# Halves of TensorE's columns in a recurrence, single weight buffers, and a first chunk in small pieces

## The chip, the core and the metric

The kernel runs on one core of a Trainium2 chip. TensorE (PE in the profile; its weight loads are PEld) multiplies, ScalarE (ACT) and VectorE (DVE) prepare operands and take results out of PSUM, GpSimd (POOL) helps with elementwise work, and SyncE (SP) issues nearly all DMAs. The metric is the device time of one execution in microseconds, as the median of several runs. All weights and inputs lie in HBM, and are float32.

## What is computed

One layer of a hybrid decoder block on 256 tokens of 2048 features. Cut to what matters:

```python
h = rmsnorm(x, norm_mix_g)
u = h @ w_in                                   # 2048 x 12288, ten fields
ya = b_g * causal_dwconv3(c_g * xa) * silu(za) # short convolution branch
o  = hgrn2_chunked(silu(q), kk, iv, log_f)     # gated linear recurrence, 8 heads of 128
yb = rmsnorm_per_head(o) * silu(og)
m  = sigmoid(ga) * (ya @ w_a_out) + sigmoid(gb) * (yb @ w_b_out)
x  = x + m @ w_o
x  = x + sigmoid(rmsnorm(x) @ w_ple_gate) * (p @ w_ple_proj)
return rmsnorm(x, final_norm_g)
```

The product of p, (256 x 256) by (256 x 2048), is the only one that needs no other result, and the kernel begins with it.

## The kernel before, in words

**The stream of weights.** Every weight matrix is cut by the host into groups of 512 output columns, and each group into chunks of 256 rows. A chunk is one *position* of a stream: a tile of 128 partitions by 1024 float32 (512 KB), whose left and right 512 columns belong to two blocks of 128 rows. `steps` (lines 139 to 144) lists the positions in order: four for p's projection (PP 0 to 3, one chunk each), then w_in with w_a and w_b between its last groups, then w_o and w_ple_gate.

**One position.** `load` (line 94) has SP fetch the raw float32 chunk; raw tiles hold two positions (1 MB), and there are three of them. `split` (line 113) makes two operands of a chunk: ScalarE rounds it to `whi` (line 124), VectorE subtracts to get the remainder `wlo` (line 125). The activations are kept as such a pair as well: `put_p` (line 905) makes p's with a cast and a subtraction on VectorE, `put_x` (line 839) x's. `product` (line 952) issues three matmuls per block of 128 rows and half of the tokens: hi by hi, hi by lo, lo by hi (line 957). So a position is twelve matmuls with 512 columns each. Two banks of PSUM hold the two halves of the tokens.

**The order of the work.** The main loop (line 960) walks the positions. At each it splits positions up to three ahead (line 971), issues the twelve matmuls, asks for the weight tiles up to AHEAD = 4 further on (line 1007), and lets each pending epilogue take one step (`advance`). From position 1 to 4 the splits are held behind the eviction of an earlier product (line 970). Epilogues write to DRAM and read back turned (`turned`, lines 233 and 235), also on SP's queue, so these stand in one line with the weight loads.

**The beginning.** SP fetches p whole (line 154, 256 KB), then the right half of position 0 (line 111, 256 KB; its left half goes out on ScalarE's queue), position 1 (512 KB), the parameters `prm` (line 158, 36 KB), and then positions 2 to 5 and the first chunks of x in turn (lines 827 to 829). Meanwhile TensorE runs ten matmuls on zeros (WARM, line 836), which VectorE has just written (line 833). Position 0 is split in two halves of 512 columns (line 973), after its half of p. Its first block issues its matmuls in the order hi by hi, lo of p by hi, hi by lo of the weights (line 1000); all other blocks go through the three kinds for one half of the tokens and then for the other.

**The recurrence.** For each of two groups of four heads (`hgrn`, line 351) small products within blocks of 128 tokens are made by `products` (line 385): at level B, key rows r multiply query columns c. Each product uses a strip of 32 of TensorE's 128 columns (`quarters`, line 378, yields r in strips of 32; `tile_position=(0, r)` places it). At level 128 a strip covers 64 query columns, at all others 32. Line 519 makes the products between the two blocks in the same manner, with 128 query columns for each strip of 32. These operands are plain float32, and each such matmul appears in the profile as two instructions.

Of the kernel before, what the change touches and what calls it, by code (L numbers as in the profile page):

```python
# [15 lines left out]
P = 128  # L16
# [10 lines left out]
WARM = 10  # L27
# [17 lines left out]
def hybrid_kernel(ctx, tc, xT, x, pT, prm, gfin, masks, w_in, w_a, w_b, w_o, w_pg, w_pp, out):  # L45
# [48 lines left out]
    def load(pos):  # L94
        w, g, c = stream[pos]
        if pos // 2 not in loaded:
            raw = wp.tile([P, 2, 2 * CW], F32, tag="raw", bufs=3, name=nm("raw"))
            loaded[pos // 2] = raw
            if FIRST <= pos < FIRST + 4:
                for i in range(2):  # L100
                    nc.sync.dma_start(out=raw[:, i, :], in_=w[g, :, c + i, :])
            elif pos >= FIRST:
                nc.sync.dma_start(out=raw, in_=w[g, :, c : c + 2, :])
        return loaded[pos // 2]

    def load_first(pos, queues):

        w, g, c = stream[pos]
        n = 2 * CW // len(queues)
        for i, eng in enumerate(queues):  # L110
            eng.dma_start(out=load(pos)[:, pos % 2, i * n : (i + 1) * n], in_=w[g, :, c, i * n : (i + 1) * n])

    def split(pos, halves=(0, 1)):
        w, g, c = stream[pos]
        src = load(pos)[:, pos % 2, :]
# [7 lines left out]
        s = slice(halves[0] * CW, (halves[-1] + 1) * CW)  # L123
# [25 lines left out]
    LEAD, AHEAD = 3, 4  # L149
# [4 lines left out]
    nc.sync.dma_start(out=praw.rearrange("p (k t) -> p k t", k=2), in_=pT)  # L154
# [3 lines left out]
    nc.sync.dma_start(out=prm_t, in_=prm)  # L158
# [192 lines left out]
    def hgrn(j):  # L351
# [26 lines left out]
        def quarters(B):  # L378

            for r in range(0, P, 32):  # L380
                c = {128: (r // 64 ^ 1) * 64, 64: r ^ 32}.get(B, r)
                n = max(B // 2, 32)
                yield slice(r, r + 32), slice(c, c + n)

        def products(bk, key, query, B, at=None):

            for h in range(4):
                for r, c in quarters(B):
# [131 lines left out]
        for h in range(4):  # L520
            for r in range(0, P, 32):
                nc.tensor.matmul(  # L522
                    heads(bo)[r : r + 32, h, :], X[:, 0, h, r : r + 32], X[:, 1, h, :], start=True, stop=True,
                    tile_position=(0, r),
                )
# [301 lines left out]
    for c in range(4):  # L827
        load_first(c + 2, (nc.sync,))
# [3 lines left out]
    warm = pools["tmp1"].tile([P, 4, P], F32, tag="both", bufs=1, name="warm")  # L832
    nc.vector.memset(warm[:, :2, :], 0.0)
# [302 lines left out]
```

## Time and profile before

| | |
|---|---|
| time, median of 3 runs | 826.04 us (825.71 to 826.06) |
| the profiled execution, its own time | 826.27 us |
| its span, first to last instruction | 824.5 us |
| mean granted TensorE clock | 0.996 |
| HBM read, written | 172.92 MB, 13.63 MB |

The span is shorter than the execution's own time by 1.8 us, which lie before the first and after the last instruction. An instruction's row in a timeline gives its start in us from the beginning of the span, its length in us, the engine and the line, what it writes and reads, and how many neighbouring instructions of the same kind were merged into the row; in square brackets stands how long the engine had been idle and what released it. SPq and ACTq are the queues on which SP and ACT issue DMAs. Matmul durations overlap: a matmul of 512 columns lasts 0.39 us in its row, while the next one starts some 0.23 us after it.

### The profile page before, as it was taken

How to read it: one execution, taken by the hardware profiler on the slowest of the kernel's cores; microseconds unless marked ns; L12 is line 12 of the kernel's file. 1: busy time of each engine (PE TensorE's matmuls, PEld its weight loads, DVE VectorE, ACT ScalarE, POOL GpSimd, SP SyncE). 2: the span in 40 equal slices, each digit the busy share in tenths (PEclk: the TensorE clock that was granted, in tenths of full speed). 3: DMA queues.
4: the chain of work that ended last, by engine and by line, in shares of the span. 5: the costliest groups of instructions: out<-in, count | busy, mean ns of one | idle time of the engine just before them, and what ended most of it. 6: DMA issues, size and time to landing. Idle time of an engine off the chain costs nothing.

```text
span 824.5 us, 10669 instructions
## 1 busy us (share of the span) xinstructions
PE 814.2 (99%) x4186; PEld 673.6 (82%) x4186; DVE 531.5 (64%) x618; ACT 432.9 (53%) x557; POOL 90.7 (11%) x74
## 2 busy tenths in 40 slices
PE   9999999999999999999999999999999999999995
PEld 6888888888888888888888888888888888888885
DVE  6747698967766588877645546545544656679633
ACT  7667465555564465466443443544444455566522
POOL 1000045300000064200001001000000000001210
PEclk9999999999999999999999999999999999999998
DMA  9969656648776565748656755756755788887702
GB/s 342 378 254 337 221 186 209 217 151 260 256 229 229 200 204 163 246 156 283 207 182 188 262 188 174 254 200 204 246 181 191 249 291 279 302 296 270 295 1 104
DMA packets 40660, 187.27 MB, mean 227 GB/s; under 512 B 4640, under 2 KB 14112, under 8 KB 22432
## 3 DMA queue, kind: packets, MB, share of 16 engines
q1 hardware_dynamic: 40176, 185.52, 65.8%
q10 hardware_dynamic: 432, 1.05, 0.3%
q8 instruction: 33, 0.54, 0.3%
q14 instruction: 19, 0.16, 0.1%
HBM read 172.92 MB, written 13.63 MB: 226 GB/s over the span
## 4 chain that ended last, share of the span: by engine, by line
PE 96%; issue 1%; DMA 1%; DVE 0%; ACT 0%; SPq 0%; POOLq 0%; POOL 0%
PE g L957 94%; PE s L389 1%; PE s L957 1%; DMA raw<-in_w_pp 1%; PE s L522 0%; PE s L546 0%; PE s L545 0%; PE s L544 0%; ACT xs L782 0%; DVE wlo L125 0%; ACT whi L124 0%; DVE t L753 0%; DVE t L757 0%; DVE xs L756 0%; POOLq L1131 0%
## 5 line engine op out<-in xcount | busy, mean ns | idle before, releaser
L125 DVE TENSOR_TENSOR wlo<-raw,whi 128x1024 fp32r<-128x1024 f32 (+1 forms) x293 | 368.0, 1261 | 254.4 <-ACT whi L124 253.8
L124 ACT ACTIVATE whi<-raw 128x1024 fp32r<-128x1024 f32 (+1 forms) x293 | 307.6, 1056 | 334.4 <-PE g L957 294.6
L957 PE MATMUL g<-whi,xl 128*128 128x512 f32 (+1 forms) x912 | 351.4, 385 | 0.0
L957 PE MATMUL g<-wlo,xh 128*128 128x512 f32 (+1 forms) x912 | 351.4, 385 | 0.0
L957 PE MATMUL g<-whi,xh 128*128 128x512 f32 (+1 forms) x912 | 351.3, 386 | 0.0
L957 PEld LDWEIGHTS g<-whi,xh 128*128 128x128 f32 x912 | 171.3, 188 | 34.7 <-issue 0.4
L957 PEld LDWEIGHTS g<-whi,xl 128*128 128x128 f32 x912 | 171.3, 188 | 34.3
L957 PEld LDWEIGHTS g<-wlo,xh 128*128 128x128 f32 x912 | 171.3, 188 | 34.1
L957 PE MATMUL g<-whi,mh 128*128 128x512 f32 x128 | 49.8, 390 | 0.0
L957 PE MATMUL g<-wlo,mh 128*128 128x512 f32 x128 | 49.7, 389 | 0.0
L957 PE MATMUL g<-whi,ml 128*128 128x512 f32 x128 | 49.5, 390 | 0.0
L677 POOL TENSOR_TENSOR t<-ga,gb 128x512 f32<-128x512 f32 x6 | 10.6, 1786 | 198.3 <-DVE gb L672 198.3
L957 PEld LDWEIGHTS g<-whi,mh 128*128 128x128 f32 x128 | 24.0, 188 | 5.3 <-ACT mh L683 0.3
L957 PE MATMUL g<-wlo,yaTh 128*128 128x512 f32 x72 | 28.0, 392 | 0.1
L957 PEld LDWEIGHTS g<-whi,ml 128*128 128x128 f32 x128 | 23.9, 188 | 5.1 <-DVE ml L684 0.2
L957 PEld LDWEIGHTS g<-wlo,mh 128*128 128x128 f32 x128 | 24.0, 188 | 5.0
L957 PE MATMUL g<-whi,yaTl 128*128 128x512 f32 x72 | 27.9, 389 | 0.0
L443 POOL TENSOR_TENSOR t<-b 128x512 f32<-128x512 f32 x10 | 20.4, 2035 | 68.1 <-DMA t<-turn 41.0
L957 PE MATMUL g<-whi,yaTh 128*128 128x512 f32 x72 | 27.8, 391 | 0.0
L957 PE MATMUL g<-whi,ybTh 128*128 128x512 f32 x64 | 24.9, 389 | 0.0
L957 PE MATMUL g<-wlo,ybTh 128*128 128x512 f32 x64 | 24.9, 389 | 0.0
L957 PE MATMUL g<-whi,ybTl 128*128 128x512 f32 x64 | 24.9, 389 | 0.0
(157 smaller groups left out, 516.5 us busy)
## 6 DMA issues: line engine op xcount, KB each, us to landing
raw<-in_w_in SPq DMA_DIRECT2D x93, 1024.0 KB, 5.1
raw<-in_w_o SPq DMA_DIRECT2D x16, 1024.0 KB, 5.9
raw<-in_w_pg SPq DMA_DIRECT2D x16, 1024.0 KB, 5.6
turn<-t SPq DMA_DIRECT2D x72, 128.0 KB, 2.6
t<-turn SPq DMA_DIRECT2D x18, 512.0 KB, 5.2
raw<-in_w_a SPq DMA_DIRECT2D x8, 1024.0 KB, 5.2
raw<-in_w_b SPq DMA_DIRECT2D x8, 1024.0 KB, 5.1
raw<-in_w_in SPq DMA_DIRECT2D x6, 512.0 KB, 7.8
```

Source lines behind the costliest of these rows:

```text
L124: a = nc.scalar.activation(out=hi[:, s], in_=src[:, s], func=AF.Copy)
L125: v = nc.vector.tensor_tensor(out=lo[:, s], in0=src[:, s], in1=hi[:, s].bitcast(F32), op=ALU.subtract)
L389: nc.tensor.matmul(heads(bk)[r, h, c if at is None else slice(at, at + 32)], key(h)[:, r], query(h)[:, c], start=True, stop=True, tile_pos ...
L443: nc.gpsimd.tensor_tensor(out=er, in0=br, in1=ref, op=ALU.subtract)
L677: (nc.vector if j == 3 else nc.gpsimd).tensor_tensor(out=spread(m, t), in0=blocks(ga[:, s]), in1=blocks(gb[:, s]), op=ALU.add)
L957: nc.tensor.matmul(psum, a, b, start=first and n == 0, stop=last and n == 2)
```

## The change

Three edits, with some that follow from them.

- **Recurrence.** `quarters` becomes `places`: at level 128 the strip is 64 of TensorE's columns instead of 32, so there are two products per head instead of four; levels 64 and below keep strips of 32. The products between the two blocks (line 519) use strips of 64 as well.
- **Weight buffers.** Six raw tiles of one position (512 KB) in place of three of two (1 MB), and one DMA per position throughout. The distance AHEAD becomes 5.
- **The beginning.** p is fetched in two halves of 128 KB, position 0 in four pieces of 128 KB, over SP's and ScalarE's queues by turns; position 1 in two pieces of 256 KB on SP's. `prm` goes out after position 2. Position 0 is split in pieces of 256, 256 and 512 columns, position 1 in two of 512. The second half of p is prepared only after the first two pieces are split. The first block of position 0 makes its matmuls for 256 columns at a time (twelve of 256 in place of six of 512). TensorE's warming-up is seven matmuls instead of ten, on a constant of ones that the program holds anyway, and VectorE's memset for it goes.

```diff
-WARM = 10
+WARM = 7
+EARLY = {0: ((0, CW // 2), (CW // 2, CW), (CW, 2 * CW)), 1: ((0, CW), (CW, 2 * CW))}
...
     def load(pos):
         w, g, c = stream[pos]
-        if pos // 2 not in loaded:
-            raw = wp.tile([P, 2, 2 * CW], F32, tag="raw", bufs=3, name=nm("raw"))
...
+        if pos not in loaded:
+            raw = loaded[pos] = wp.tile([P, 2 * CW], F32, tag="raw", bufs=6, name=nm("raw"))
+            if pos >= FIRST:
+                nc.sync.dma_start(out=raw, in_=w[g, :, c, :])
+        return loaded[pos]
...
-    LEAD, AHEAD = 3, 4
+    LEAD, AHEAD = 3, 5
...
-    nc.sync.dma_start(out=praw.rearrange("p (k t) -> p k t", k=2), in_=pT)
-    load_first(0, (nc.scalar, nc.sync))
-    load_first(1, (nc.sync,))
+    load_p(0)
+    n = CW // 2
+    load_columns(0, 0, n, nc.scalar)
+    load_columns(0, n, CW, nc.sync)
+    load_p(1, nc.scalar)
+    load_columns(0, CW, CW + n, nc.sync)
+    load_columns(0, CW + n, 2 * CW, nc.scalar)
+    for n in range(2):
+        load_columns(1, n * CW, (n + 1) * CW, nc.sync)
...
-            for r in range(0, P, 32):
-                c = {128: (r // 64 ^ 1) * 64, 64: r ^ 32}.get(B, r)
-                n = max(B // 2, 32)
-                yield slice(r, r + 32), slice(c, c + n)
+            n = max(B // 2, 32)
+            for r in range(0, P, n):
+                c = r ^ n if B > 32 else r
+                yield slice(r, r + n), slice(c, c + n)
...
-            for r in range(0, P, 32):
+            for r in range(0, P, 64):
                 nc.tensor.matmul(
-                    heads(bo)[r : r + 32, h, :], X[:, 0, h, r : r + 32], X[:, 1, h, :], start=True, stop=True,
+                    heads(bo)[r : r + 64, h, :], X[:, 0, h, r : r + 64], X[:, 1, h, :], start=True, stop=True,
                     tile_position=(0, r),
                 )
...
     for c in range(4):
-        load_first(c + 2, (nc.sync,))
+        load_columns(c + 2, 0, 2 * CW, nc.sync)
+        if c == 0:
+            nc.sync.dma_start(out=prm_t, in_=prm)
         load_x(c)
...
-    nc.vector.memset(warm[:, :2, :], 0.0)
...
+    ones = [nc.const_aps.tensor(1.0, [P, n], mybir.dt.bfloat16) for n in (P, CW)]
...
-            if done == 0:
-                for i in range(2):
-                    put_p(i)
-                    split(done, (i,))
-            else:
+            for c0, c1 in EARLY.get(done, ((0, 2 * CW),)):
+                if done == 0 and c0 % CW == 0:
+                    with ExitStack() as first:
+                        for i in state["splits"] if c0 else ():
+                            first.enter_context(tc.issue_after(i))
+                        put_p(c0 // CW)
                 for k in range(2 * (done - 4), min(2 * (done - 4) + 2, KT)) if done >= 4 else ():
                     put_x(k)
-                split(done)
+                split(done, c0, c1)
...
-            s = slice(i * CW, (i + 1) * CW)
-            for n in ((0,), (2,), (1,)) if pos == 0 and i == 0 else ((0, 1, 2),):
-                for t in range(NT):
-                    product(psum[t], state[opname], k, t, hi[:, s], lo[:, s], k == 0, k == 2 * nch - 1, n)
+            for c0, c1 in EARLY[0][:2] if pos == 0 and i == 0 else ((0, CW),):
+                s = slice(i * CW + c0, i * CW + c1)
+                for n in ((0,), (2,), (1,)) if pos == 0 and i == 0 else ((0, 1, 2),):
+                    for t in range(NT):
+                        product(
+                            psum[t][:, c0:c1], state[opname], k, t, hi[:, s], lo[:, s], k == 0 and c0 == 0, k == 2 * nch - 1, n
+                        )
```

More of the change, by code (lines that the diff above doesn't have):

```diff
@@ L95, in load, with split @@
         w, g, c = stream[pos]
[L96 to L115 removed]
+        if pos not in loaded:
[3 more added lines that the diff above has]
+        return loaded[pos]
+    def split(pos, c0=0, c1=2 * CW):
+        w, g, c = stream[pos]
+        src = load(pos)
         pool, n = (pools["late"], 6) if (pos - state.get("late", len(steps))) % 10 < 6 and "late" in state else (wp, 4)
```

17 lines of the change are left out of this document (9 added, 8 removed).

## The prediction

> **What bounds the kernel now.** I read the page first, for the engine that is full, then the chain of waits in order of time, for the places where that engine is held up, and then the timeline of those places.
>
> ```profile
> span 824.5 us, 10669 instructions
> PE 814.2 (99%) x4186; PEld 673.6 (82%) x4186; DVE 531.5 (64%) x618; ACT 432.9 (53%) x557; POOL 90.7 (11%) x74
> ```
>
> TensorE is busy for 814.2 of 824.5 us. So a change counts only if it lets TensorE start its real products earlier, spares it a stall, or changes the length of what it does. The chain says where these are:
>
> ```profile
> 1.65 5.18 DMA raw<-in_w_pp
> ...
> 6.85 1.07 ACT whi L124
> ...
> 7.94 1.24 DVE wlo L125
> ...
> 9.22 2.57 PE g L957 x10
> 11.79 5.44 PE s L957 x24
> 17.23 119.68 PE g L957 x528
> ...
> 162.92 1.01 PE s L522 x32
> ...
> 176.70 0.22 PE s L544 x2
> ```
>
> Up to 9.22 us the end is set by the landing of position 1 and its two conversions; from there on the chain runs on TensorE until the tail. A product takes 119.68 / 528 = 0.227 us. The change touches two places of this chain: the stretch before 11.63 us, where position 2 begins, and the recurrence's small products.
>
> **The beginning.** The timeline of the first 12 us, weight loads and other queues left out:
>
> ```profile
> 1.19 4.38 PE L837 MATMUL s<-warm 128*128 128x512 bf16 x10 [1.19 <-DVE warm L833]
> ...
> 4.69 0.49 DVE L909 CAST yaTh<-t 128x256 fp32r<-128x256 f32 x2 [3.56 <-DMA t<-in_pT]
> ...
> 4.87 1.29 ACT L124 ACTIVATE whi<-raw 128x512 fp32r<-128x512 f32 x2 [2.19 <-DMA raw<-in_w_pp]
> ...
> 5.54 0.69 DVE L125 TENSOR_TENSOR wlo<-raw,whi 128x512 fp32r<-128x512 f32 x1
> ...
> 5.55 0.73 PE L957 MATMUL g<-whi,yaTh 128*128 128x512 f32 x2
> ...
> 6.48 0.68 DVE L125 TENSOR_TENSOR wlo<-raw,whi 128x512 fp32r<-128x512 f32 x1
> ...
> 7.27 0.44 PE L957 MATMUL g<-wlo,yaTh 128*128 128x512 f32 x1
> ...
> 8.26 1.06 ACT L124 ACTIVATE whi<-raw 128x1024 fp32r<-128x1024 f32 x1 [0.35 <-DMA raw<-in_w_pp]
> ...
> 8.48 0.63 PE L957 MATMUL g<-whi,yaTh 128*128 128x512 f32 x2
> ...
> 9.22 0.50 PE L957 MATMUL g<-wlo,yaTh 128*128 128x512 f32 x1
> ...
> 9.35 1.23 DVE L125 TENSOR_TENSOR wlo<-raw,whi 128x1024 fp32r<-128x1024 f32 x1 [0.18 <-ACT whi L124]
> ...
> 9.56 0.39 PE L957 MATMUL g<-whi,yaTl 128*128 128x512 f32 x1
> ...
> 11.63 0.39 PE L957 MATMUL s<-whi,yaTh 128*128 128x512 f32 x1
> ...
> 11.86 0.39 PE L957 MATMUL s<-wlo,yaTh 128*128 128x512 f32 x1
> ```
>
> VectorE and ScalarE begin when p and the first 512 columns have landed, 4.69 and 4.87. From then VectorE works almost without a break until 6.48 + 0.68 = 7.16, when the second block's remainder is there; the product at 7.27 needs it. The next product that waits is that of 9.22: its predecessor started at about 8.48 + 0.23 = 8.71, so it could have started at 8.94. It lost 0.28 there, and the next start came 0.34 after it instead of 0.23, another 0.11.
>
> *Landing.* 512 KB had to land before the two could work; now 256 KB do.
>
> ```profile
> 3.00:4.00 1.00, 1.00 (x4) 0.32 (x3) 0.00 (x0) 0.00 (x0) 0.00 (x0) 1.00 0.91 336
> 4.00:5.00 1.00, 1.00 (x3) 0.30 (x2) 0.31 (x2) 0.13 (x1) 0.00 (x0) 1.00 1.09 428
> ```
>
> The last column is GB/s: 0.26 MB less at 336 to 428 GB/s is 0.61 to 0.78 us. The rows of a piece are half as long, 1 KB, and no row shows their speed: if a packet of 1 KB took as long as one of 2 KB, nothing would be gained. Bounds 0 and 0.78; I take 0.65, near the rate that is measured. So VectorE begins at 4.04 and ScalarE at 4.22.
>
> *VectorE to the second block.* It does the same work as in its 7.16 − 4.69 = 2.47 us, only that one subtraction of 512 columns (0.69) becomes two of 256.
>
> ```profile
> L752 ACT ACTIVATE t<-g,r2r 128x256 f32<-128x256 f32 x4 | 1.8, 473 | 13.4 <-PE g L957 13.4
> L753 DVE TENSOR_TENSOR t<-t,pw 128x256 f32<-128x256 f32 x4 | 1.6, 426 | 14.0 <-ACT t L752 14.0
> ```
>
> By the nearest operations of 256 columns, that is 2 x 0.43 − 0.69 = 0.17 more. The second 256 columns land 256 KB later, 4.22 + 0.65 = 4.87, and are rounded by 5.34, while VectorE gets there at about 4.04 + 0.25 + 0.42 + 0.43 = 5.14; part of that wait stays, and I add 0.10. The remainder is there at 4.04 + 2.47 + 0.17 + 0.10 = 6.78, so 0.38 sooner, and the product of 7.27 moves to 6.89. That p's second half is now kept behind the first two splits costs nothing beyond this, since its cast stands in the sum. TensorE has the twelve narrower products (by their width no longer together than the six) done in its waiting time, from about 4.7.
>
> *Position 1.* It now comes in halves. The left half's remainder follows at 6.78 + 0.69 = 7.47; TensorE asks for it after 0.34 and five more products of 0.227, at about 8.4. The right half lands as all of it did, by 6.85 (the bytes ahead of it are the same), is rounded in 1.29 / 2 = 0.65 and subtracted in 0.69, so 8.2; it is asked for near 9.75. The stall of 9.22 is gone, with both its parts: 0.39.
>
> *What is late next.* Position 2 would begin at 11.63 − 0.38 − 0.39 = 10.86 and ask for its remainder at 11.09. This is there at 9.35 + 1.23 = 10.58, if position 2 lands when it did. So at most 11.86 − 10.58 = 1.28 can be gained at all. But its transfer goes out later:
>
> ```profile
> 0.74 0.38 SPq L154 DMA_DIRECT2D t<-in_pT  x1
> ...
> 2.59 0.60 SPq L111 DMA_DIRECT2D raw<-in_w_pp  x1
> ...
> 4.87 0.33 SPq L822 DMA_DIRECT2D t<-in_xT  x1
> ```
>
> From the first of these rows up to the last, eight transfers went out, ScalarE's one among them; the last row is the ninth, and it left only after the first had landed. The change puts eight small ones ahead of position 2 (the row of 2.59), so its transfer becomes the ninth and goes out at about 4.1. Of the 1.3 MB ahead of it, 0.34 MB have moved from 3 to 4 us and some 0.2 before; the rest is nearly 2 us of work, so I expect no gap, and count nothing; `prm` no longer goes ahead of it. If all of the 1.5 us showed, the remainder would come at 12.1 and TensorE would lose 0.2. Beyond position 2 the next landings and conversions have more room. The term of the beginning is **−0.77**, taken as −0.75, bounds −1.28 and +0.2.
>
> Also moved: ScalarE issues three DMAs instead of one ahead of its table load and first activation.
>
> ```profile
> 0.73 0.41 ACTq L111 DMA_DIRECT2D raw<-in_w_pp  x1
> ...
> 1.18 1.28 ACT L167 ACT_TABLE_LOAD   x1 [1.18 <-PEq L1125]
> ...
> 2.47 0.21 ACT L167 ACTIVATE table<-mhalf 128x8 f32<-128x8 f32 x1
> ```
>
> Two more at 0.45 put the end of the last at 2.68 + 0.9 = 3.6, still ahead of 4.22. If landings came sooner than 3.6 this would hold the rounding up.
>
> **Six single buffers.** The same bytes per position, 512 KB per DMA instead of 1 MB. SP issues some 130 more, at 0.33 us each; it is not on the chain after 9.22, and a position takes 12 x 0.227 = 2.72 us. A wait is added on every position where there was one on every second, for the remainder of the position six back; behind it stand the turned stores and loads of the epilogues. That remainder is made while TensorE is still one position behind, and the load of before waited for the same one, so nothing is delayed beyond one position. I count 0. TensorE works three positions, 8 us, behind the splits; that is the cover.
>
> **The recurrence.** One burst of it:
>
> ```profile
> 162.53 0.39 PE L957 MATMUL g<-whi,xl 128*128 128x512 f32 x1
> 162.85 1.08 PE L522 MATMUL s<-X 128*32 128x128 f32 x32
> 163.75 0.93 PE L389 MATMUL s<-X 128*32 128x64 f32 x64
> 164.52 0.75 PE L389 MATMUL s<-qT,kT 128*32 128x32 f32 x64
> 165.21 0.50 PE L957 MATMUL g<-whi,xh 128*128 128x512 f32 x1
> 165.54 0.40 PE L957 MATMUL g<-wlo,xh 128*128 128x512 f32 x1
> ```
>
> Line 522 issues 32 instructions in 163.75 − 162.85 = 0.90 us, 0.11 for four. The chain's row at 176.70 has two full-width float32 instructions with as many query columns in 0.22, 0.11 each. So four strips run side by side in the time of one, and what costs is the number of columns that stream through. Two strips of 64 take their 0.11 as well: sixteen instructions fewer here and sixteen at level 128 save nothing. What is added is one change from strips of 64 to strips of 32 per burst. Entering and leaving strips costs 162.85 − 162.53 − 0.23 = 0.09 and 165.54 − 165.21 − 0.23 = 0.10. For the inner change, not in the trace, the bounds are 0 and 0.19; I take 0.10, for two bursts **+0.20**.
>
> The Trainium skill speaks against this edit: by its page TensorEngine Tiling (Array Packing), section Tiling Modes, a change of the mode, not merely of the tile, drains TensorE. The extra starts agree with it in kind; with a drain the forecast stands, without one it would be 825.3.
>
> **Sum.** 826.27 − 0.75 + 0.20 = 825.72 for an execution like the profiled one, which lies 0.23 above the median of 826.04; so **825.5**.
>
> **Rivals.** *TensorE stays slow longer.* The ten warming products start 0.43 apart (4.38 / 10), the real ones 0.23 apart from 5.55 on, 4.36 us after the first. Seven take 3.0 us, and then nothing comes until 4.7. If TensorE must be busy for 4.36 us anew, it is slow until 9.06: between 6.89 and then 5 products pass instead of 9.6, a loss of 1.0, and the time is 826.5. For it: only 3.0 us of warming and a gap. Against it: the start is earlier by the memset, and the first products follow within a microsecond. 13%. The Trainium skill, page TensorE: Matmul & The Clock Gate, Part 1, has the full rate granted after a busy window of about 3.4 us that runs free of the kernel; by that, 3.0 us do not suffice by themselves, which leans to this rival.
>
> *The halves of 64 run one after the other.* Then line 522 takes twice its 0.90, and level 128, some two thirds of the 0.77 from 163.75 to 164.52 where the next kind begins, twice its 0.5: 1.4 per burst, 2.8 in all, and 828.3, slower. It comes out as slower from 2.2 of these 2.8 on, that is if four fifths of the overlap are lost. Against it: strips of 32 do run together. 7%.
>
> *The landings don't move* (time per packet, or position 2 late): the beginning gives nothing, 826.2. 10%.
>
> *All of it works out*, 1.28 at the beginning and no inner change: 824.7. 5%.
>
> The forecast has 65%, from 825.0 to 826.0. The range 824.7 to 826.7 takes in all but the second rival and what I have not thought of. A measurement of this kernel can tell some 0.2%, 1.65 us, from no change; only rivals beyond it count as faster (below 824.4) or slower (above 827.7).
>
> **What would show it.** Right: the cast starts near 4.0, the first real product near 4.7, no gap at position 1, position 2 near 10.9; bursts of unchanged length plus 0.1. Wrong: products 0.43 apart after 6.9, a gap ahead of position 2, line 522 taking 1.8 us, or waits on DMA in the middle of the span.

## The result, and the profile after

| | before | changed |
|---|---|---|
| time, median of 22 runs each | 825.9 us (825.48 to 826.75) | 826.8 us (825.64 to 828.59) |
| ratio, with its 95% interval | | 1.0014 (1.0008 to 1.0019) |
| the profiled execution, its own time | 826.27 us | 828.43 us |
| its span and mean granted clock | 824.5 us, 0.996 | 826.5 us, 0.995 |

The changed kernel was 0.9 us slower, 1.3 above the forecast and 0.1 above the end of the range. The difference is smaller than the 0.2% that the prediction set as the least that can be told. The 22 runs of the changed kernel fall in two bunches, and both are in the median: fifteen from 825.64 to 827.01 (median 826.63, 0.7 above before) with a mean clock of 0.996 to 0.998, and seven from 828.05 to 828.59 with 0.994 or 0.995. The profiled execution is one of the seven. A second comparison, made later (e6 below), had one of eleven in the upper bunch and a median 0.4 below the kernel before.

The page of the changed kernel, first the span and the busy time of each engine:

```profile
span 826.5 us, 10940 instructions
PE 815.5 (99%) x4125; PEld 675.5 (82%) x4125; DVE 532.5 (64%) x619; ACT 433.8 (52%) x559; POOL 89.5 (11%) x74
```

TensorE is as full as it was, and its 61 instructions fewer are busy for 1.3 us more. The chain of waits in order of time says where:

```profile
1.66 5.17 DMA raw<-in_w_pp
6.85 0.64 ACT whi L115
7.51 0.70 DVE wlo L116
8.26 5.87 PE g L961 x17
14.13 5.44 PE s L961 x24
19.57 119.68 PE g L961 x528
...
178.92 0.22 PE s L548 x2
```

It has the form of before's chain: a landing, a rounding, a subtraction, then TensorE to the end. But position 2 begins at 14.13 rather than 11.79, later and not sooner. The row of 528 products then starts 19.57 − 17.23 = 2.34 later, and lasts as long to the hundredth. At the normalisation behind the first burst the lag is 178.92 − 176.70 = 2.22. So all of the loss arises in the first 14 us, and a little is won back at the recurrence.

TensorE's timeline of these 14 us:

```profile
0.77 3.15 PE L841 MATMUL s<-const-bfloat16-1.0 128*128 128x512 bf16 x7 [0.77 <-PEq L1135]
4.01 0.80 PE L961 MATMUL g<-whi,yaTh 128*128 128x256 f32 x2
...
5.98 0.40 PE L961 MATMUL g<-wlo,yaTh 128*128 128x256 f32 x2
7.53 0.49 PE L961 MATMUL g<-whi,yaTh 128*128 128x512 f32 x1 [1.15 <-ACT whi L115]
8.26 0.50 PE L961 MATMUL g<-wlo,yaTh 128*128 128x512 f32 x1 [0.23 <-DVE wlo L116]
...
9.31 0.63 PE L961 MATMUL g<-wlo,yaTh 128*128 128x512 f32 x1
...
12.29 0.44 PE L961 MATMUL g<-whi,yaTl 128*128 128x512 f32 x1
12.58 0.39 PE L961 MATMUL g<-whi,yaTh 128*128 128x512 f32 x1
```

The first real product starts at 4.01, 1.54 sooner than before. The twelve narrow products are through by 6.4, and then TensorE is idle for 1.15 us, and again for 0.23, until the second block's operands are there. From 9.31 to 12.29 the products start 0.43 apart, twice the usual 0.23. Who is late is seen in ScalarE's timeline:

```profile
6.85 1.80 ACT L115 ACTIVATE whi<-raw 128x512 fp32r<-128x512 f32 x3 [2.06 <-DMA raw<-in_w_pp]
9.36 1.06 ACT L115 ACTIVATE whi<-raw 128x1024 fp32r<-128x1024 f32 x1 [0.71 <-DMA raw<-in_w_pp]
```

ScalarE waits 2.06 us for the right half of position 0, whose last piece landed at 6.83 (the chain's first row, 1.66 + 5.17); before, it had been there by 5.51 (the second of the two roundings that start at 4.87). The table by stage, with GB/s in the last column and the busy share of the DMA engines in the one before it:

```profile
2.00:3.00 1.00, 1.00 (x4) 0.43 (x3) 0.00 (x0) 0.85 (x1) 1.00 (x3) 1.00 0.96 264
3.00:4.00 1.00, 0.92 (x3) 0.01 (x1) 0.64 (x3) 0.94 (x3) 0.28 (x2) 1.00 0.83 264
4.00:5.00 1.00, 0.99 (x4) 0.99 (x5) 0.59 (x3) 0.42 (x1) 0.00 (x0) 1.00 0.82 274
```

From 3 to 5 us the DMA engines move 264 and 274 GB/s, where they moved 336 and 428 in the same two stretches of before; from 2 to 3 us they move more, 264 against 152. From 2 to 5 us that is 0.80 MB against 0.92. Three stretches chosen by the granted clock (the third column from the right) show what the idle time brought with it:

```profile
5.50:9.00 3.50, 2.12 (x11) 1.41 (x11) 1.49 (x3) 1.78 (x3) 0.00 (x0) 1.00 1.01 340
9.00:12.40 3.40, 3.40 (x10) 2.64 (x9) 1.97 (x3) 2.03 (x3) 0.00 (x0) 0.50 1.03 402
12.40:15.80 3.40, 3.40 (x17) 2.77 (x16) 2.67 (x4) 3.40 (x8) 0.00 (x0) 1.00 1.04 402
```

TensorE was busy for 2.12 of 3.50 us; for the 3.40 us behind that it had a granted clock of 0.50, and then 1.00 again. Ten products took the place of seventeen there, a loss of 7 x 0.23 = 1.6 us.

The burst, by TensorE's timeline of the changed kernel:

```profile
165.21 1.09 PE L526 MATMUL s<-X 128*64 128x128 f32 x16
166.14 1.02 PE L393 MATMUL s<-X 128*64 128x64 f32 x48
166.97 0.80 PE L393 MATMUL s<-qT,kT 128*32 128x32 f32 x64
167.70 0.50 PE L961 MATMUL g<-whi,xh 128*128 128x512 f32 x1
168.04 0.40 PE L961 MATMUL g<-wlo,xh 128*128 128x512 f32 x1
```

Sixteen instructions of strips of 64 start in 166.14 − 165.21 = 0.93 us, 32 of strips of 32 took 0.90. From the first of the burst to the second product behind it pass 168.04 − 165.21 = 2.83 us, 2.69 before. So the burst itself costs 0.14 more, near the 0.10 that was forecast. The addition is spread over its kinds: 0.03 in the first, 0.06 in the second (166.97 − 166.14 = 0.83 against 0.77), 0.04 in the last (0.73 against 0.69). That it is the price of the one change of strips is therefore not shown. At the second burst, near 345 us, it is 0.07 (2.83 against 2.76). What wins it back is found 1.3 us behind the burst. Before's timeline there:

```profile
166.47 0.40 PE L957 MATMUL g<-whi,xl 128*128 128x512 f32 x1
166.87 0.51 PE L957 MATMUL g<-whi,xh 128*128 128x512 f32 x1
167.21 0.40 PE L957 MATMUL g<-wlo,xh 128*128 128x512 f32 x1
```

These starts lie 0.40 and 0.34 apart, where 0.23 is usual: TensorE stood for 0.28 us. Nothing of the kind follows the changed kernel's burst, and in before itself nothing follows the second burst: the products behind it start 0.23 apart.

### The profile page after: what moved, and what is told of

Its sections match the earlier page's. It is cut to its first block, busy times and chain, and to the rows that moved or that the text cites. A ratio compares the mean times of both kernels' runs of the same rounds, so it can differ in the third digit from the quotient of the medians.

```text
span 826.5 us, 10940 instructions
## 1 busy us (share of the span) xinstructions
PE 815.5 (99%) x4125; PEld 675.5 (82%) x4125; DVE 532.5 (64%) x619; ACT 433.8 (52%) x559; POOL 89.5 (11%) x74
## 4 chain that ended last, share of the span: by engine, by line
PE 97%; issue 1%; DMA 1%; DVE 0%; ACT 0%; ACTq 0%; DVEq 0%; POOLq 0%; POOL 0%
PE g L961 94%; PE s L393 1%; PE s L961 1%; DMA raw<-in_w_pp 1%; PE s L526 0%; PE s L549 0%; PE s L550 0%; PE s L548 0%; DVE t L757 0%; DVE wlo L116 0%; DVE t L761 0%; DVE xs L760 0%; DVEq L1141 0%; ACT whi L115 0%; DVE xs L788 0%
## 5 line engine op out<-in xcount | busy, mean ns | idle before, releaser
L961 PE MATMUL g<-whi,yaTh 128*128 128x512 f32 (+1 forms) x74 | 29.3, 400 | 1.2 <-ACT whi L115 1.2
L961 PE MATMUL g<-wlo,yaTh 128*128 128x512 f32 (+1 forms) x74 | 29.1, 398 | 0.2 <-DVE wlo L116 0.2
L961 PE MATMUL g<-whi,yaTl 128*128 128x512 f32 (+1 forms) x74 | 28.9, 396 | 0.0
```

The lines of the kernel that those rows point to most:

```text
L961: nc.tensor.matmul(psum, a, b, start=first and n == 0, stop=last and n == 2)
```

## The experiments

Several theories were left after the result. **Theory A:** the small pieces land at a lower rate, the second block's operands are late, and the idle time lowers TensorE's clock; the recurrence adds its 0.2. **Rivals:** the strips of 64 or the single buffers cost the time in the middle of the span. Each median below stands beside that of the kernel before on the same chip.

### One part alone

**e1, the strips alone** (before, with the changed recurrence):

```diff
-            for r in range(0, P, 32):
-                c = {128: (r // 64 ^ 1) * 64, 64: r ^ 32}.get(B, r)
-                n = max(B // 2, 32)
-                yield slice(r, r + 32), slice(c, c + n)
+            n = max(B // 2, 32)
+            for r in range(0, P, n):
+                c = r ^ n if B > 32 else r
+                yield slice(r, r + n), slice(c, c + n)
```

(and the same strips on the products between the blocks)

> The kernel before, with only the recurrence's strips of 64 columns. Theory (each burst pays one more change of strip width, and the strips run side by side as before): the burst that begins with line 522 lasts 0.07 to 0.14 us longer in each of the two groups, line 522 itself still 0.90 us, and the time is 0.1 to 0.3 us above the kernel before. Rival (the two halves run partly one after the other): line 522 takes 1.2 us or more, and the time is 0.7 us or more above. Rival (the loss of the whole change lies in the recurrence): the full 0.9 us of the change appears here.

Measured: 826.23 (826.06 to 826.48) beside 826.21, ratio 1.0 (0.9991 to 1.0009). The burst is 0.14 longer, as in the changed kernel, and the pause behind it is gone, as there. The two cancel: 0.14 and 0.07 more in the two bursts, 0.28 less in the one pause.

**e2, the six single buffers alone:**

```diff
-            raw = wp.tile([P, 2, 2 * CW], F32, tag="raw", bufs=3, name=nm("raw"))
+            raw = loaded[pos] = wp.tile([P, 2 * CW], F32, tag="raw", bufs=6, name=nm("raw"))
...
-    LEAD, AHEAD = 3, 4
+    LEAD, AHEAD = 3, 5
```

> The kernel before, with only the six single buffers, one DMA of 512 KB per position, and AHEAD of 5; the beginning's transfers as before. Theory: nothing that bounds the kernel is touched, so the time is within 0.2 us of the kernel before, and every execution shows the same clock as before (0.996). Rival (the added waits on SP's queue delay the turned loads, and with them the conversions): TensorE shows new gaps after 20 us, and the time is 0.3 us or more above.

Measured: 826.82 (826.04 to 828.16), ratio 1.0008 (1.0 to 1.0017). No DMA was waited for in the middle of the span. What was longer is the pause behind the burst, by TensorE's timeline of this run:

```profile
166.73 0.40 PE L953 MATMUL g<-whi,xl 128*128 128x512 f32 x1
167.41 0.50 PE L953 MATMUL g<-whi,xh 128*128 128x512 f32 x1 [0.28 <-issue]
```

The starts lie 0.68 apart instead of 0.23, and the next one follows 0.34 later: a pause of 0.56, counted as before's 0.28 was. The releaser is "issue": TensorE waits for no operand and no bank that the profile shows. The longer pause accounts for 0.28 of the 0.6, and the spans are longer by as much (median 824.6 beside 824.3); the rest lies outside the span, where this run has 2.0 us and the kernel before 1.8, and has no explanation.

**e3, the changed kernel with strips of 32:**

```diff
-            n = max(B // 2, 32)
-            for r in range(0, P, n):
-                c = r ^ n if B > 32 else r
-                yield slice(r, r + n), slice(c, c + n)
+            for r in range(0, P, 32):
+                c = {128: (r // 64 ^ 1) * 64, 64: r ^ 32}.get(B, r)
+                n = max(B // 2, 32)
+                yield slice(r, r + 32), slice(c, c + n)
...
```

> The changed kernel with the recurrence put back to strips of 32; the buffers and the new beginning stay. Theory (the beginning makes the loss: the last pieces of position 0 land late, and in some executions TensorE falls back to half its clock after the gap): the times fall in two bunches as with the whole change, one 0.3 to 0.7 us above the kernel before, one 1.5 to 2 us above that with a mean clock lower by 0.002, and the median is 0.1 to 0.3 us below that of the whole change. Rival (the strips make the loss): the time is at or below the kernel before.

Measured: 827.59 (827.15 to 828.11), ratio 1.0017 (1.0008 to 1.0026). Without the strips of 64 the kernel is slower, against what was expected. In its TensorE timeline the pause has grown to 1.77 − 0.23 = 1.54 us, and with the start behind it (0.34 later) to 1.65:

```profile
165.34 0.40 PE L961 MATMUL g<-wlo,xh 128*128 128x512 f32 x1
167.11 0.50 PE L961 MATMUL g<-whi,xl 128*128 128x512 f32 x1 [1.37 <-issue]
```

Its beginning, the same as the changed kernel's, went better: the right half landed by 5.9, TensorE waited for 0.22 us only, the clock was not lowered in any of its eleven runs, and the row of 528 products started at 17.05, 0.18 sooner than before. Its table by stage:

```profile
2.00:3.00 1.00, 1.00 (x4) 0.44 (x3) 0.00 (x0) 0.85 (x1) 1.00 (x3) 1.00 0.95 297
3.00:4.00 1.00, 0.92 (x3) 0.01 (x1) 0.61 (x2) 0.94 (x3) 0.28 (x2) 1.00 1.16 309
4.00:5.00 1.00, 0.99 (x4) 1.00 (x5) 0.93 (x4) 0.42 (x1) 0.00 (x0) 1.00 1.04 320
```

From 2 to 5 us that is 0.93 MB, as much as before's 0.92, and still the right half landed 0.4 later than before's 5.51. So a lower rate is not the whole reason why the small pieces land late. Bytes that stand behind them in the queue, position 1 first, must have moved among them: in the changed kernel 1.1 MB had moved by 6.0 us without the right half's last bytes, and p and position 0 are 0.79 MB together.

**e12, the buffers and the strips, with the beginning of before** (the edits of e1 and e2 together):

> The kernel before with the single buffers and the strips of 64, and the beginning as before. Theory (what the single buffers cost by themselves, 0.6 us, is the longer wait for instructions after the recurrence's burst, which strips of 64 avoid): no gap after the burst, and 826.1 to 826.4, 0.4 to 0.7 below the single buffers alone. Rival (they cost by delaying transfers elsewhere): 826.7 or more, with gaps elsewhere.

Measured: 826.14 (825.99 to 826.6) beside 826.22, ratio 1.0 (0.9991 to 1.0009). The products behind the burst start 0.23 apart throughout. So with strips of 64 no cost of the single buffers shows; what they cost inside the span with strips of 32 was the longer pause. No gain shows either (e10).

### What the pause behind the burst is

TensorE issues as many weight loads as matmuls, 2 x 4186 instructions before. The page counts the packets on the queue of instructions (packets, MB, share):

```profile
q8 instruction: 33, 0.54, 0.3%
```

0.54 MB in 33 packets are 16 KB each, and 2 x 4186 instructions in 33 are some 250 each, so that the blocks look to be TensorE's. In a burst they run out faster than anywhere else, so the theory is that TensorE gets ahead of its own instructions there.

The times of these packets fit it. One moved from 164.01 to 165.56 us in before, from 165.10 to 166.09 in e2, from 164.65 to 165.61 in e3 and from 164.78 to 165.74 in e8 (below), and TensorE went on 1.3 to 1.5 us after its end in all four. Behind the second burst, near 347 us, none of the four has a pause, and there no such packet moved between 338 and 349 us. So the pause follows one of the two bursts, not each.

**e8, the changed kernel with the query columns halved**, so that the strips stay and the instructions come back:

```diff
+                for c2 in (0, 32) if B == 128 else (None,):
                     for r, c in places(B):
+                        if c2 is not None:
+                            c = slice(c.start + c2, c.start + c2 + 32)
...
+            for c2 in (0, 64):
                 for r in range(0, P, 64):
...
```

> The changed kernel, with strips of 64 as there, but each product of line 526 made in two halves of 64 query columns, and each of level 128 in two of 32: as many instructions as with strips of 32, and no more columns in all. Theory (after the recurrence's burst TensorE waits for its own instructions, because a burst of many short ones uses them up faster than they are fetched): a gap of 0.3 to 1.7 us comes back within 3 us after the first burst's end near 165 us, and the time is 0.3 to 1.5 us above the changed kernel. Rival (the gap belongs to strips of 32, or to the conversions): no gap after the burst, and the time within 0.2 us of the changed kernel.

Measured: 827.91 (827.05 to 828.78) beside 826.26, ratio 1.0018 (1.0009 to 1.0027). TensorE's timeline:

```profile
162.83 1.15 PE L530 MATMUL s<-X 128*64 128x64 f32 x32
163.81 1.47 PE L396 MATMUL s<-X 128*64 128x32 f32 x64
165.10 0.80 PE L396 MATMUL s<-qT,kT 128*32 128x32 f32 x64
...
166.16 0.40 PE L965 MATMUL g<-wlo,xh 128*128 128x512 f32 x1
167.18 0.50 PE L965 MATMUL g<-whi,xl 128*128 128x512 f32 x1 [0.63 <-issue]
```

The pause is back with the instructions: the starts lie 167.18 − 166.16 = 1.02 us apart, a pause of 0.79, where the strips of 64 alone had none. The time is 2.1 above the changed kernel on the same chip (e6, 825.84), more than the 0.3 to 1.5 expected, since the bursts grew too, by 0.5 each. So the pause goes by the number of instructions and not by the width of the strips. The burst itself went from 2.83 to 166.16 − 162.83 = 3.33 us. Nearly all of that is at level 128, 165.10 − 163.81 = 1.29 against 0.83, although the columns that stream through are as many. That the pause is the fetch of a block fits e1, e2, e3, e8 and e12 and the times of the packets; that it is just this fetch was not isolated.

### The beginning

**e4 and, on another chip, e7: the changed kernel with six unused products** behind the first block, which keep TensorE busy while it waits (their result is not used):

```diff
+            if pos == 0 and i == 0:
+                with tc.issue_after(state["made"]):
+                    for _ in range(6):
+                        nc.tensor.matmul(wb, *ones, start=True, stop=True)
```

(and `product` keeps its last matmul as `state["made"]`)

> The changed kernel with six products on the constant of ones put behind the first block of position 0, where TensorE stood idle for 1.15 us; their result is not used, and nothing is left out. Theory (idling at the beginning lets the clock fall back to half for 3.4 us in some executions): the upper bunch of times, 828.0 to 828.6, is gone, no stretch of the first 15 us has a clock of 0.5 after the first full-rate product, and the median is 0 to 0.5 us below that of the whole change. Rival (the upper bunch comes from later landings, and the clock only follows): some executions still lie 1.5 us or more above the others. Against both: if the pieces land sooner in other executions, the six products themselves delay the second block by up to 0.7 us.

Measured (e4): 826.54 (825.73 to 826.88) beside 826.21, ratio 1.0002 (0.9993 to 1.0011). TensorE's timeline has the filling, and later products 0.23 apart:

```profile
5.70 1.48 PE L1016 MATMUL s<-const-bfloat16-1.0 128*128 128x512 bf16 x6
...
8.12 0.39 PE L961 MATMUL g<-wlo,yaTh 128*128 128x512 f32 x1
8.35 0.40 PE L961 MATMUL g<-whi,yaTl 128*128 128x512 f32 x1
```

**e6, the changed kernel once more**, on the chip of e7:

> The changed kernel once more, beside the others on one chip. Theory (idling of TensorE at the beginning, met by the clock's window in some executions): about a third of the executions lie near 828.4 with a clock lower by 0.002, the others near 826.6. Rival (the upper bunch belonged to the chip that it ran on): one bunch only, near 826.6.

> The changed kernel with six unused products behind the first block of position 0, once more, now beside the changed kernel itself. Theory (idling lets the clock fall): no execution near 828.4, while the changed kernel on the same chip has some. Rival: as many upper executions as the changed kernel has.

Measured: e6 825.84 (825.21 to 828.35) beside 826.26, ratio 0.9997 (0.9988 to 1.0005); e7 826.29 (825.43 to 826.82), ratio 0.9997 (0.9988 to 1.0006). One of e6's eleven runs was at 828.35 with a clock of 0.995, where a third was expected, and the others lay around 825.8 rather than 826.6. In the two comparisons 8 of 33 runs of the changed kernel had a mean clock of 0.995 or less, all of them above 828; of the filled kernels' 22 none had, and of the 119 runs of the kernel before that lay beside the experiments none either. That fits the theory that the idle time lowers the clock. The counts alone do not show it: e3 and e8 have the same beginning without filling, and none of their 22 runs had the lower clock, so that 8 of 55 stand against 0 of 22, and on the chips of the experiments 1 of 33. The filling shows no gain in the median, and by itself leaves the second block as late.

In e6's profiled execution the right half landed late as well, by 6.75, TensorE waited 0.79 and 0.22, and the clock stayed:

```profile
5.90:9.30 3.40, 2.39 (x10) 1.60 (x10) 1.87 (x4) 1.80 (x4) 0.00 (x0) 1.00 1.01 359
```

2.39 busy of 3.40 kept it, 2.12 of 3.50 did not. The clock records in the changed kernel's trace change at 5.55, 8.97 and 12.38, each 3.41 us after the other. Counted in steps of 3.41 us from the first record of the full clock, TensorE was idle for 1.38 us in the changed kernel's step from 5.55 to 8.97, for 1.01 in e6's from 6.19 to 9.60, and for 0.91 at most in such a step of any other profile here, up to 15 us. Only the first lost the clock. One profile is no proof, but it is the one with the most idle time. The first record lies anywhere from 3.81 to 6.67 in the profiles (e10 apart), so the same idle time can fall into one step or be divided between two, and a part of the runs is what one would expect.

**e5, the changed kernel with a beginning in pieces of 256 KB** (p whole, position 0 in halves of 512 columns, ten warming products; strips, buffers and position 1 in halves as in the changed kernel):

```diff
-WARM = 7
-EARLY = {0: ((0, CW // 2), (CW // 2, CW), (CW, 2 * CW)), 1: ((0, CW), (CW, 2 * CW))}
+WARM = 10
+EARLY = {0: ((0, CW), (CW, 2 * CW)), 1: ((0, CW), (CW, 2 * CW))}
...
-    load_p(0)
-    n = CW // 2
-    load_columns(0, 0, n, nc.scalar)
-    load_columns(0, n, CW, nc.sync)
-    load_p(1, nc.scalar)
-    load_columns(0, CW, CW + n, nc.sync)
-    load_columns(0, CW + n, 2 * CW, nc.scalar)
+    nc.sync.dma_start(out=praw.rearrange("p (k t) -> p k t", k=2), in_=pT)
+    load_columns(0, 0, CW, nc.scalar)
+    load_columns(0, CW, 2 * CW, nc.sync)
...
```

> The changed kernel with the beginning's transfers in rows of 2 KB again: p whole, position 0 in two halves of 256 KB (ScalarE's and SP's queue), converted in two halves, ten warming products; position 1 in two halves, prm after position 2, the single buffers and the strips of 64 stay. Theory (rows of 1 KB make the transfers slow, so that the second half of position 0 lands no sooner than before): the first product starts 1.5 us later than in the changed kernel, near 5.55, yet the second block's remainder is there near 7.1 as before; there is no gap of more than 0.3 us up to 12 us, the clock never falls to 0.5, and the time is 0.2 to 0.5 us below the kernel before. Rival (the size of the pieces is not it, the order of the queues is): the second half of position 0 lands later than 5.8, and the time is at or above the kernel before.

Measured: 825.92 (825.38 to 827.76) beside 826.26, ratio 0.9996 (0.9987 to 1.0005). The table by stage of this run:

```profile
3.00:4.00 1.00, 1.00 (x4) 0.30 (x3) 0.00 (x0) 0.00 (x0) 0.28 (x2) 1.00 1.00 375
4.00:5.00 1.00, 1.00 (x3) 0.15 (x1) 0.61 (x2) 0.47 (x1) 0.00 (x0) 1.00 1.10 410
```

375 and 410 GB/s with rows of 2 KB, in the stretches in which the changed kernel moved 264 and 274 and e3 309 and 320. The right half is there by 5.05 and nothing waits behind the first product at 5.21. The length of the rows is not all that differs: p and position 0 come in three transfers instead of six, and one of them instead of three goes over ScalarE's queue. On that queue a row of 1 KB cost at most about a tenth more per byte: up to 7 us it took 16.4% of the DMA engines' time for 0.39 MB in the changed kernel, 9.9% for 0.26 MB before. Of the change's edit to the beginning, position 1 in halves, `prm` behind position 2 and the constant of ones are left here, and the row of 528 starts some 0.8 sooner than before. Less than half of that is in the time: the spans are 0.6 shorter than before's by their medians (823.8 against 824.4), and 2.2 us lie outside the span instead of 1.8. Why is not known.

**e10, e5 with the pair buffers of before:**

```diff
-            raw = loaded[pos] = wp.tile([P, 2 * CW], F32, tag="raw", bufs=6, name=nm("raw"))
+            raw = wp.tile([P, 2, 2 * CW], F32, tag="raw", bufs=3, name=nm("raw"))
...
-    LEAD, AHEAD = 3, 5
+    LEAD, AHEAD = 3, 4
...
```

> Strips of 64 and the beginning in rows of 2 KB (p whole, position 0 in two halves, position 1 in two halves, prm after position 2, ten warming products), with the three buffers of two positions and DMAs of 1 MB as in the kernel before. Theory (the single buffers bring nothing; the halves of position 1 remove the second stall, the strips remove the wait for instructions): 825.2 to 825.7, 0.5 to 1.0 below the kernel before, and no execution 1.5 us above the others. Rival (the single buffers carry the gain of the kernel with 256 KB pieces): at or above 826.0.

Measured: 825.9 (825.63 to 827.73) beside 826.22, ratio 0.9998 (0.999 to 1.0007). It missed the 825.2 to 825.7 that was expected. It is what e5 was on another chip, so no gain of the single buffers shows. The profiled execution (827.69) is one of two upper ones, and its mean clock is 0.998, so it is another matter than the changed kernel's upper bunch. Its TensorE timeline:

```profile
3.29 1.91 PE L841 MATMUL s<-const-bfloat16-1.0 128*128 128x512 bf16 x4
5.72 1.22 PE L961 MATMUL g<-whi,yaTh 128*128 128x512 f32 x2 [0.52 <-ACT whi L119]
...
9.29 0.58 PE L961 MATMUL g<-whi,yaTl 128*128 128x512 f32 x1
9.71 0.40 PE L961 MATMUL g<-whi,yaTh 128*128 128x512 f32 x1
```

The warming ended at 5.20, 0.52 us of idle followed, and the products went 0.43 apart up to 9.7: the full rate was not lost here, it came 3.4 us late. The trace's first record of the full clock is at 9.69. In the step of 3.41 us that ended at 6.27 TensorE was idle for these 0.52 us, and the full clock was not granted; in e9 it was granted after a step with 0.38 idle.

**e13, e5 with twelve warming products instead of ten:**

```diff
-WARM = 10
+WARM = 12
```

> The kernel with 256 KB pieces (single buffers, strips of 64) with twelve warming products in place of ten, so that TensorE no longer idles for 0.6 to 0.7 us between the last of them and the first product. Theory (some executions start at half the clock until near 9.7 us because that pause falls into the window that decides): no execution 1.5 us above the others, where four of 22 with ten products were near 827.7; the quick executions stay within 0.3 us of 825.8. Rival (the upper executions have another cause, such as late landings): again one or two of eleven near 827.7.

Measured: 825.83 (825.37 to 826.33) beside 826.09, ratio 0.9998 (0.9989 to 1.0007). The warming now runs up to the first product without idle time:

```profile
0.78 4.48 PE L837 MATMUL s<-const-bfloat16-1.0 128*128 128x512 bf16 x12 [0.78 <-PEq L1131]
5.22 0.73 PE L957 MATMUL g<-whi,yaTh 128*128 128x512 f32 x2
```

None of 11 runs was above 826.4, against 4 of 22 of e5 and e10 above 827.6. That agrees with the theory; with so few runs it doesn't show it (the kernel before had 4 of 119 above 827.4).

**e9, the last 128 KB of position 0 sent after position 2**, which was to widen the idle time:

```diff
-    load_columns(0, CW + n, 2 * CW, nc.scalar)
...
+            load_columns(0, CW + CW // 2, 2 * CW, nc.sync)
```

> The changed kernel, with the last 128 KB of position 0 sent out on SP's queue behind position 2, so that TensorE idles some 3 to 4 us instead of 1 before the second block. Theory (a clock window of 3.4 us in which TensorE mostly idles halves the clock for the next one): the later landing alone gives about 829; nearly every execution, not one in seven, has the lower mean clock (0.993 to 0.995), the profile shows a stretch of about 3.4 us at 0.5 after the gap, and the time is near 830.5. Rival (the lower clock of some executions is chance and has nothing to do with the gap): the mean clock stays at 0.996 to 0.998 in most executions and the time is near 829.

Measured: 826.46 (826.0 to 828.03) beside 826.22, ratio 1.0002 (0.9993 to 1.0011). It missed its aim: position 1's products came first and filled the time, and TensorE was idle for no longer than 0.62 us. One of eleven runs had a clock of 0.994. It decides nothing.

**e11, the changed kernel with the right half of position 0 in one piece of 256 KB**, the left half still in two of 128:

```diff
-    load_columns(0, CW, CW + n, nc.sync)
-    load_columns(0, CW + n, 2 * CW, nc.scalar)
+    load_columns(0, CW, 2 * CW, nc.sync)
```

> The changed kernel with only the right half of position 0 sent as one piece of 256 KB on SP's queue, in place of two of 128 KB over two queues. Theory (the rows of 1 KB and the share of the second queue make this half late): it lands by 5.7 instead of 5.9 to 6.8, the gap after the first block is below 0.6 us, no execution has the lower clock, and the time is 0.2 to 0.6 us below the changed kernel's quick executions, 825.2 to 825.7. Rival (the transfers ahead of it are what makes it late): it lands after 5.9, and the time is that of the changed kernel.

Measured: 825.66 (825.33 to 826.74) beside 826.22, ratio 0.9992 (0.9983 to 1.0001), the lowest median of all. TensorE's timeline:

```profile
4.00 0.80 PE L960 MATMUL g<-whi,yaTh 128*128 128x256 f32 x2
...
6.74 0.73 PE L960 MATMUL g<-whi,yaTh 128*128 128x512 f32 x2 [0.62 <-ACT whi L115]
```

The time is what the theory said, and the landing is what the rival said: the right half landed by 6.03, although it came in rows of 2 KB on SP's queue alone, and from 3 to 5 us the engines moved 297 and 283 GB/s. So this run speaks against the length of its rows as the reason why it is late. One idle time of 0.62 stays; none of eleven runs had a lowered clock. The interval takes in 1, so that it beats the kernel before is not shown.

**e14, e11 with four unused products** in that idle time (the edit of e4 with `range(4)`; their result is not used):

> The changed kernel with the right half of position 0 in one piece of 256 KB, and four unused products behind the first block of position 0, which fill 0.9 us of its gap. Theory (the early start is worth something once the gap neither grows nor lowers the clock): 825.3 to 825.8, no execution above 827.5, and the best of all the kernels here by its median. Rival (the filling products delay the second block as much as they save): 0.3 us or more above the same kernel without them, 825.66.

Measured: 826.1 (825.79 to 826.5) beside 826.09, ratio 0.9999 (0.999 to 1.0008). The rival was right, 0.44 above e11's 825.66: the filling stands in the way of real products. No kernel here is shown to be faster than the kernel before.

## Why the prediction was wrong, step by step

- **Landing.** It took 256 KB less at 336 to 428 GB/s and said itself that no row showed the speed of rows of 1 KB. The first pieces came even sooner than its bound of 0.78 allowed: cast 3.32 instead of 4.04 (1.37 before the old 4.69), first product 4.01 instead of 4.7. They had 264 GB/s from 2 to 3 us, where before had 152. From 3 to 5 us the rate fell to 264 and 274 GB/s (309 and 320 in e3); e5 with rows of 2 KB had 375 and 410. The Trainium skill, page DMA: Bandwidth & Descriptors, section Specifications, puts the least transfer for the full rate at 512 B. The runs do not settle whether that holds here: the kernels with rows of 1 KB had the lower rates from 3 to 5 us, but e11 had 297 and 283 with half of position 0 in rows of 2 KB, so that the number of transfers and their order stay as rivals.
- **VectorE to the second block: the step that failed.** It forecast 6.89 for the product on the remainder, taking the engine for the limit, and gave the right half of position 0 no landing time at all: the wait for it stood in the sum at nothing. That landing was the limit. It came at 6.83 in the changed kernel's profile, 6.75 in e6 and 5.9 in e3, against 5.51 before, and the product started at 8.26, 8.18 and 7.33. Before had 7.27. So this term was not −0.38 but between +0.06 and +1.
- **Position 1.** Its stall is gone where it lands in time (e3, e5), as forecast. In e3 the two terms together are the −0.18 at the row of 528 products, where −0.77 was said. That its right half lands by 6.85 because the bytes ahead of it are the same was wrong: even its left half's rounding in e3 had to wait for a landing until 7.15.
- **What is late next.** ScalarE waited for position 2 until 9.36, 1.1 later than before (8.26), and TensorE asked for it only at 14.13. That its later transfer would not show was right; TensorE came late itself.
- **TensorE stays slow longer.** This rival, at 13%, was near in its price (1.0, measured 1.6 where it happens) and wrong in its mechanism. The full clock came at 5.55 in the changed kernel's profile, before's at 5.36, and the products of 5.98 already ran at the full rate. The seven warming products did not bring that by themselves: the narrow real products, which follow 0.09 us behind them, filled the rest of the 3.41 us before it. What the rival describes happened only where idle time came between, in one profile of e10. What the prediction left out is that idle time can take the full clock away again: in this profile 1.4 us of it were followed by 3.41 us at half the clock. The Trainium skill, page TensorE: Matmul & The Clock Gate, Part 1, has the lower clock after at least one idle window of about 3.4 us. The length of the window agrees with the 3.41 us here; that a whole window must be idle does not, since one with 2.12 us of work in 3.50 was enough in this one profile.
- **The recurrence, +0.10 a burst.** Right in size: +0.14 at the first, +0.07 at the second. That it is one change of strips is not shown, since the addition lies in all three kinds of the burst. Strips of 64 run side by side, 0.93 us where 1.8 was the rival's; that rival is dead. Wrong was that "sixteen instructions fewer here and sixteen at level 128 save nothing": they save the pause behind the first burst, 0.28 us before and 1.65 in e3, so that the edit comes to nothing alone (e1) and is needed with single buffers.
- **Six single buffers at 0.** Right only with the strips of 64 (e12); with strips of 32 they cost 0.6 (e2), half of it by the pause and not by the wait that was weighed, the other half outside the span.

In sum, for a profiled execution the beginning gives between −0.2 (e3) and some +0.7 (e6, and the changed kernel without the loss of clock), instead of −0.75, and the recurrence about −0.1 (e1: 0) instead of +0.2. The lowered clock adds about 1.6 to 8 of the changed kernel's 33 runs. That the median came out only 0.1 above the range is luck: it is made of two bunches, and neither comes from the sum that was forecast.

**Open.** In the first comparison the changed kernel is slower by 0.9, in the second faster by 0.4 with an interval that takes in 1, so the sign is not settled. The right half landed anywhere from 5.3 to 6.8 in profiles of the same beginning (5.3 in e7, 5.9 in e3, 6.8 in e6 and the first); why is not known, and neither is what makes the small pieces slow: rows, transfers or order. Nor is why single buffers lengthen the pause behind the burst: more transfers on the same DMA engines are a guess.

## What to carry to other kernels

Smaller first pieces brought the first operand sooner and what stood behind it later: work out when the last piece that the first two blocks need lands, not only the first one. Idle time right after the start can cost more than itself, by the clock: 1.38 us did, 1.01 did not. A later start without gaps had none of its eleven runs above 826.4 (e13), though its median is not shown to be better. And in a burst of very short matmuls count the instructions as well as the columns, and look up to two microseconds behind the burst for idle time put down to "issue".

## What was not expected of the hardware

- With the first pieces in rows of 1 KB the engines moved 264 and 274 GB/s (309 and 320 in e3), and with rows of 2 KB in fewer transfers 375 and 410 (e5), in the same two stretches.
- The granted clock fell to 0.50 for 3.41 us after a stretch with TensorE idle for 1.4 of 3.5 us, and not after one with 1.0 of 3.4. It came 3.4 us late (9.7) where the warming left 0.52 us idle ahead of the first product.
- TensorE paused for 0.3 to 1.65 us shortly behind the first of two bursts of 320 instructions, weight loads included, and did not with 64 fewer. It went on 1.3 to 1.5 us after a packet of 16 KB on the queue of instructions had ended.
- Halving the columns of the level-128 products, 64 to 32, took 0.46 us more per burst for the same columns. Strips of 32 at 32 columns start 64 instructions in 0.73 us, 11 ns apart. The Trainium skill, page TensorE: Matmul & The Clock Gate, Part 1, has a floor of about 25 ns from start to start; with strips side by side this trace goes below it.
